# A state space layer's tables M, loaded from overlapping parts of K's rows instead of from a DRAM copy of their own

## The chip, the core and the metric

The kernel runs on one core of a Trainium2 chip. The metric is the device time of one execution in microseconds (us). Five engines work side by side, each in the order of its own instruction list: TensorE (PE; its weight loads are shown as PEld), VectorE (DVE), ScalarE (ACT), GpSimd (POOL) and SyncE (SP). SP does no arithmetic here, it only issues DMAs. Sixteen DMA engines move the data, whichever engine issues the transfer.

## What is computed

A decoder trunk of two layers on 256 tokens of 2048 features, in float32. Layer 0 mixes tokens with a causal convolution module, layer 1 with a state space layer (SSM) that ends in a gated linear unit. Each is followed by a squared-ReLU MLP with 8192 hidden features. The SSM is the part that the change touches:

```python
def ssm_module(h, lam_re, lam_im, log_dt, b_re, b_im, c_re, c_im, d_skip, w_glu):
    u = h.astype(f32).reshape(bsz, L, SSM_GROUPS, SSM_GROUP)      # 128 groups of 16 channels
    ...
    bu_re = jnp.einsum("blgc,gpc->blgp", u, bb_re)                # 64 complex states per group
    ...
    _, _, s_re, s_im = lax.associative_scan(combine, (a_re, a_im, bu_re, bu_im), axis=1)
    y = (jnp.einsum("blgp,gcp->blgc", s_re, c_re.astype(f32))
         - jnp.einsum("blgp,gcp->blgc", s_im, c_im.astype(f32)))
    y = y.reshape(bsz, L, D_MODEL) + d_skip.astype(f32) * h.astype(f32)
    y = jax.nn.gelu(y).astype(h.dtype)
    z = y @ w_glu
    val, gate = jnp.split(z, 2, axis=-1)
    return val * jax.nn.sigmoid(gate)
```

## The kernel before

**The large products.** Every float32 weight is split into a rounded part `hi` and a rest `lo`, and three products are summed on TensorE. Weights come in steps (`add_t`, `add_f`); a step is two halves of 512 KB. `load` (line 105) has SP issue the DMA of a half into a buffer `raw`, of which there are six (line 127). `split` (line 144) makes `hi` on ACT and `lo` on DVE, with four buffers each (line 153). Then TensorE uses the half. `fetch` (line 100) makes every DMA on SP stand behind the fetch before it, so SP's order is the order in which the program asks. A DMA on SP also waits until the one eight places before it has landed.

**The SSM in chunks.** The 256 tokens are cut into 32 chunks of 8 tokens. For each group of 16 channels there are three constant tables of 128 rows by 128 columns: W takes the 8 x 16 inputs of a chunk to the 64 complex states, V takes the carried state to the 8 x 16 outputs, and M takes the inputs of a chunk to the outputs of the same chunk. M depends only on the distance between two tokens. Its row for token offset d (16 rows, one for each channel c) is a window of a longer row K[g, c] of 15 x 16 numbers, and the windows of neighbouring offsets overlap: columns d*16 to d*16 + 128.

**Where the tables are made.** `ssm_prep` (line 1066) puts the work that builds W, V, K and the rotation table R into a list, `bg`, which is worked off between the steps of layer 0's MLP. `kstage` (line 1317) makes K for 8 groups on TensorE, ACT and DVE and writes it to the DRAM tensor Kd of [128 groups, 16 channels, 240] with four DMAs on POOL's queue. `mstage` (line 1334) copies 16 rows of M for 32 groups from Kd to the DRAM tensor Md of [128 rows, 128 groups, 128], also on POOL's queue; with 8 offsets and 4 blocks of 32 groups that is 32 copies.

**Where the tables are used.** The 128 groups are taken in four blocks B = 0 to 3. `table` (line 1394) has SP load a table of one block, [128 partitions, 32 groups, 128 columns] or 2 MB, into one of six large buffers `blk`. The tables W0, W1, M0, V0 and R0, R1 are asked for between the last steps of layer 0's MLP (line 1827). M1, V1, W2 and R2 are asked for in `begin` (line 1585) at the start of the gated unit. The others are asked for just ahead of given steps of the gated unit (`before_load`, line 1677): W3, then M2 and R3, then V2, M3, V3. `ssm_local(B)` (line 1533) multiplies block B's inputs by M, `ssm_carry(B)` (line 1549) adds the product with V, and `ssm_out(B)` (line 1564) transposes the result for the gated unit, whose matmuls (`mm_t`, lines 268 to 270) then use it. In `begin`, `ssm_local(1)` stands on TensorE ahead of the transposes of `ssm_out(0)`; the other calls stand between steps of the gated unit (`todo`, line 1669). The tile framework adds the waits between engines, and its scheduler picks the order where the program leaves it open.

Two other loads go to fewer than 128 partitions: `xJ`, the inputs by chunks, to 32 partitions at a time in pieces of 512 B (line 1364), and in the convolution `R`, shifted rows, to 32 partitions at a time in pieces of 1136 B (line 537, on ACT's queue).

Of the kernel before, what the change touches and what calls it, by code (L numbers as in the profile page):

```python
# [10 lines left out]
F32 = mybir.dt.float32  # L11
# [8 lines left out]
P = 128  # L20
# [8 lines left out]
G, ST, GC = 128, 64, 16  # L29
CH = 8  # L30
# [7 lines left out]
class Trunk:  # L38
# [47 lines left out]
    def add(self, view, shape, consume, pre=None):  # L86
        self.steps.append((view, shape, consume, pre))
# [978 lines left out]
    def ssm_prep(self):  # L1066
        nc, a, bg = self.nc, self.a, self.bg
        add = lambda c, fn: bg.append((c, fn))
        const = self.const
        self.Wd = self.dram.tile([P, G, P], F32, name="Wd")  # L1070
        self.Kd = self.dram.tile([G, GC, 15 * GC], F32, name="Kd")
        self.Md = self.dram.tile([P, G, P], F32, name="Md")
        self.Vd = self.dram.tile([P, G, P], F32, name="Vd")
        self.Bd = self.dram.tile([G, 2, ST, GC], F32, name="Bd")
        self.Rd = self.dram.tile([P, NQ, 1024], F32, name="Rd")
# [1 line left out]
        dma = nc.gpsimd.dma_start  # L1077
# [223 lines left out]
        def vstage(k):  # L1301
            vs = s["bv"][:, 2944:4096].rearrange("p (g d c) -> p g d c", d=9, c=GC)
            g = slice(8 * k, 8 * k + 8)
            c = [s["c12"][:, i, g, :].unsqueeze(2).broadcast_to([P, 8, 8, GC]) for i in range(2)]
            p = [s[x][:, g, :].unsqueeze(3).broadcast_to([P, 8, 8, GC]) for x in ("pr", "pi")]
            v = vs[:, :, 1:9, :]
            self.tt(v, c[0], p[0], ALU.mult)
            n = 4 if k >= 14 else 8
            t = s["bv"][:, 2944 - 128 * n:2944].rearrange("p (g d c) -> p g d c", d=8, c=GC)
            for h in range(0, 8, n):  # L1310
                h = slice(h, h + n)
                self.tt(t, c[1][:, h], p[1][:, h], ALU.mult)
                s["vadd"] = self.tt(v[:, h], v[:, h], t, ALU.add)
            nc.scalar.activation(vs[:, :, 0, :], s["c12"][:, 0, g, :], AF.Copy)
            dma(out=self.Vd[:, g, :], in_=v.rearrange("p g d c -> p g (d c)"))

        def kstage(k):
            vs = s["bv"][:, 2944:4096].rearrange("p (g x) -> p g x", x=9 * GC)
            bs = s["bv"]
            ps = self.bank([P, 2, P], name="kp")  # L1320
            with self.behind(s["vadd"]), self.tc.high_priority(offset=URGENT):
                for gl in range(8):
                    q, hh = gl % 4, gl // 4
                    nc.tensor.matmul(ps[32 * q:32 * q + 32, hh, :], lhsT=bs[:, (8 * k + gl) * GC:(8 * k + gl + 2) * GC],
                                     rhs=vs[:, gl, 0:P], start=hh == 0, stop=hh == 1, skip_group_check=True)
            ks = self.t2([P, 2, P], name="ks")
            nc.scalar.activation(ks, ps, AF.Copy)
            for j in range(2):
                self.stt(ks[:, j, 0:GC], self.m32[:, 0:GC], self.dgl[:, k, j:j + 1], ks[:, j, 0:GC], ALU.mult, ALU.add)
            kd = self.Kd.rearrange("(k h q) c e -> k q c h e", k=16, h=2, q=4)  # L1330
            for q in range(NQ):
                dma(out=kd[k, q, :, :, 7 * GC:15 * GC], in_=ks[32 * q:32 * q + GC])

        def mstage(B, d):
            dma(out=self.Md[d * GC:(d + 1) * GC, 32 * B:32 * B + 32, :],
                in_=self.Kd[32 * B:32 * B + 32, :, d * GC:d * GC + P].rearrange("g c x -> c g x"))
        for k in reversed(range(16)):
            add(12, lambda k=k: vstage(k))
            add(4 if k >= 12 else 3, lambda k=k: kstage(k))
            if k < 12:  # L1340
                for d in range(2 * (k % 4), 2 * (k % 4) + 2):
                    add(0.5, lambda B=k // 4 + 1, d=d: mstage(B, d))
        for d in range(CH):
            add(0.5, lambda d=d: mstage(0, d))


    def ssm_slice(self, n):
# [46 lines left out]
    def table(self, kind, B):  # L1394

        if kind == "R":
            t = self.t4([P, 2, 16, 32], name="R") if B != 2 else self.S[:, 1]
            self.fetch(t.rearrange("p i g j -> p (i g j)"), self.Rd[:, B])
        else:
            t = self.blk_tile([P, 32, P], name=kind + "t")  # L1400
            src = {"W": self.Wd, "M": self.Md, "V": self.Vd}[kind]
            for h in range(0, 32, 16):
                self.fetch(t[:, h:h + 16, :], src[:, 32 * B + h:32 * B + h + 16, :])
        self.tables[kind, B] = t

    def ssm_block(self, b):
# [452 lines left out]
```

## Time and profile before

| | |
|---|---|
| time, median of 3 runs | 1935.12 us (1935.08 to 1935.7) |
| time of the profiled execution | 1935.06 us |
| its span, first to last instruction | 1933.3 us |
| DMA, mean over the span | 242 GB/s, 468.45 MB |
| Md<-Kd, POOL's queue | 32 DMAs of 256 KB, median 7.1 us to landing |
| Mt<-Md, SP's queue | 8 DMAs of 1024 KB, median 8.8 us to landing |
| Wt<-Wd and Vt<-Vd, SP's queue | 8 DMAs of 1024 KB each, median 9.1 and 8.1 us to landing |

The page gives the busy time of each engine as a share of the span. A view by stretches gives, for each stretch, its length, then for each engine the busy time with the count of instructions, then TensorE's clock, the busy share of the 16 DMA engines, and the GB/s they moved. Transfers overlap within an engine, so the share can come out a little over 1. A row of a DMA queue has its packets, the MB, and the time of its packets as a share of 16 engines over the stretch. A timeline row has start and length in us, engine, line, operation, and output<-input; in brackets stands idle time before it and what ended that. "Landing" is from the issue of a DMA to its completion. In a row of DMAs the three numbers are the length of the issue in ns (least, median, most), then come the first and the last start in us.

### The profile page before, as it was taken

The page shows a single profiled execution, that of the slowest core. Times are in us where ns is not written, and L with a number is a line of the kernel's source. Part 1 is how long each engine was busy: PE and PEld are TensorE (multiplying, and loading weights), DVE is VectorE, ACT ScalarE, POOL GpSimd, SP SyncE. Part 2 cuts the span into 40 slices and gives each one's busy share as a digit, 9 for nine tenths or more (in the row PEclk, how much of TensorE's full clock was granted, in tenths as well). Part 3 has the DMA queues.
Part 4 walks back from the last instruction along what each step waited for, and adds up shares of the span by engine and source line. Part 5 has one row for each costly group of instructions (what it writes and reads, how often), then busy time and mean ns, then how long its engine had stood idle before and what let it go on. Part 6 is the DMA issues. An engine that isn't in the chain of part 4 may idle for free.

```text
span 1933.3 us, 30420 instructions
## 1 busy us (share of the span) xinstructions
PE 1915.5 (99%) x11372; PEld 1641.5 (85%) x11372; DVE 1656.2 (86%) x2246; ACT 1124.9 (58%) x1405; POOL 395.6 (20%) x364
## 2 busy tenths in 40 slices
PE   8999999999999999999999999999999999999998
PEld 8999788888888888888888788888888888888887
DVE  6999798899878898988557869679999999999987
ACT  6444555554465565655545446566666666667664
POOL 3899300001021221213101001001111111111100
PEclk9999999999999999999999999999999999999999
DMA  9667468778788888888898978668998998989984
GB/s 247 186 183 217 124 209 251 220 243 270 251 205 251 238 289 233 280 225 278 280 339 302 337 247 219 195 208 229 260 265 228 266 265 239 260 252 254 247 258 145
DMA packets 338675, 468.45 MB, mean 242 GB/s; under 512 B 16801, under 2 KB 218593, under 8 KB 335169
## 3 DMA queue, kind: packets, MB, share of 16 engines
q1 hardware_dynamic: 296464, 364.69, 59.1%
q0 software_dynamic: 38496, 97.27, 21.5%
q10 hardware_dynamic: 3568, 4.56, 0.8%
q8 instruction: 89, 1.46, 0.3%
q14 instruction: 58, 0.48, 0.1%
HBM read 439.93 MB, written 34.91 MB: 246 GB/s over the span
## 4 chain that ended last, share of the span: by engine, by line
PE 96%; DVE 2%; DMA 1%; issue 0%; ACT 0%; POOL 0%; SPq 0%; POOLq 0%; DVEq 0%; ACTq 0%
PE acc L245 24%; PE acc L248 13%; PE acc L268 7%; PE acc L269 7%; PE acc L270 7%; PE mp L760 4%; PE mp L761 4%; PE mp L759 4%; PE acc L257 3%; PE acc L259 3%; PE acc L258 3%; PE acc L278 2%; PE acc L277 2%; PE acc L279 2%; PE mr L760 2%; PE mr L759 2%
## 5 line engine op out<-in xcount | busy, mean ns | idle before, releaser
L156 ACT ACTIVATE hi<-raw 128x1024 fp32r<-128x1024 f32 x634 | 670.9, 1060 | 622.2 <-PE acc L245 201.4
L163 DVE TENSOR_TENSOR lo<-raw,hi 128x1024 fp32r<-128x1024 f32 x573 | 695.6, 1221 | 184.1 <-ACT hi L156 169.7
L245 PE MATMUL acc<-hT,hi 128*128 128x512 f32 x2048 | 516.6, 392 | 0.1
L245 PEld LDWEIGHTS acc<-hT,hi 128*128 128x128 f32 x2048 | 370.8, 189 | 71.0 <-ACT hi L156 1.7
L248 PEld LDWEIGHTS acc<-hT,lo 128*128 128x128 f32 x2048 | 279.4, 190 | 21.1 <-issue 1.2
L248 PE MATMUL acc<-hT,lo 128*128 128x256 f32 x2048 | 287.0, 282 | 0.0
L156 ACT ACTIVATE hi<-sum 128x1024 fp32r<-128x1024 f32 x152 | 161.4, 1062 | 103.2 <-DVE sum L1025 26.9
L163 DVE TENSOR_TENSOR lo<-sum,hi 128x1024 fp32r<-128x1024 f32 x152 | 185.3, 1219 | 23.9 <-ACT hi L156 14.8
L123 POOL DMA_DIRECT2D sum<-in_mlp_w_down_dram x72 | 87.7, 1222 | 548.8 <-DVE v L1034 310.3
L163 POOL TENSOR_TENSOR lo<-raw,hi 128x1024 fp32r<-128x1024 f32 x60 | 144.0, 2414 | 30.2 <-ACT hi L156 24.1
L257 PE MATMUL acc<-hT,hi 128*128 128x256 f32 x512 | 146.2, 286 | 0.9 <-ACT hi L156 0.9
L259 PE MATMUL acc<-hT,lo 128*128 128x256 f32 x512 | 145.4, 286 | 0.2 <-POOL lo L163 0.2
L258 PE MATMUL acc<-hT,hi 128*128 128x256 f32 x512 | 145.5, 285 | 0.0
L1034 DVE SCALAR_TENSOR_TENSOR cv<-vT,cv 128x256 f32<-128x256 f32 x348 | 141.0, 487 | 2.6 <-ACT cv L587 2.2
L760 PE MATMUL mp<-lo,rT 128*128 128x512 f32 x288 | 112.4, 390 | 0.0
L761 PE MATMUL mp<-hi,rT 128*128 128x512 f32 x288 | 112.2, 390 | 0.0
L759 PE MATMUL mp<-hi,rT 128*128 128x512 f32 x288 | 110.4, 390 | 0.0
L257 PEld LDWEIGHTS acc<-hT,hi 128*128 128x128 f32 x512 | 98.9, 193 | 3.4 <-issue 2.1
L259 PEld LDWEIGHTS acc<-hT,lo 128*128 128x128 f32 x512 | 98.4, 193 | 1.7 <-issue 0.8
L258 PEld LDWEIGHTS acc<-hT,hi 128*128 128x128 f32 x512 | 98.8, 193 | 0.9 <-issue 0.8
L269 PE MATMUL acc<-lo,rT 128*128 128x512 f32 x240 | 93.6, 390 | 0.0
L268 PE MATMUL acc<-hi,rT 128*128 128x512 f32 x240 | 93.6, 391 | 0.0
(359 smaller groups left out, 3247.0 us busy)
## 6 DMA issues: line engine op xcount, KB each, us to landing
raw<-in_mlp_w_up_dram SPq DMA_DIRECT2D x256, 512.0 KB, 6.0
raw<-in_mlp_w_down_dram SPq DMA_DIRECT2D x220, 512.0 KB, 5.7
sum<-in_mlp_w_down_dram POOLq DMA_DIRECT2D x108, 512.0 KB, 7.8
raw<-in_conv_w_in_dram SPq DMA_DIRECT2D x128, 256.0 KB, 3.7
raw<-in_ssm_w_glu_dram SPq DMA_DIRECT2D x62, 512.0 KB, 5.0
raw<-in_conv_w_out_dram SPq DMA_DIRECT2D x32, 512.0 KB, 4.2
Vd<-bv POOLq DMA_DIRECT2D x16, 512.0 KB, 5.6
Md<-Kd POOLq DMA_DIRECT2D x32, 256.0 KB, 7.1
```

Source lines behind the costliest of these rows:

```text
L156: self.nc.scalar.activation(hi, sl, AF.Copy)
L163: ins = eng.tensor_tensor(out=lo, in0=sl, in1=hi.bitcast(F32), op=ALU.subtract)
L245: mm(accs[m], lhsT=hi[:, kk, cs[m]], rhs=xT(k0 + kk), start=first and kk == 0, stop=False)
L248: mm(accs[m][:, 0:T], lhsT=lo[:, kk, cs[m]], rhs=xT(k0 + kk)[:, 0, :], start=False, stop=last and kk == 3)
L257: mm(accs[m], lhsT=hi[:, kk, c], rhs=x[:, 0, :], start=first and kk == 0, stop=False)
L258: mm(accs[m], lhsT=hi[:, kk, c], rhs=x[:, 1, :], start=False, stop=False)
L259: mm(accs[m], lhsT=lo[:, kk, c], rhs=x[:, 0, :], start=False, stop=last and kk == 3)
L268: mm(acc[:, b, :], lhsT=ak[:, 0, t], rhs=hi[:, kk, :], start=first and kk == 0, stop=False)
L269: mm(acc[:, b, :], lhsT=ak[:, 0, t], rhs=lo[:, kk, :], start=False, stop=False)
L759: mm(lhsT=F[0], rhs=hi[:, j, :], start=first and half == j == 0, stop=False)
L760: mm(lhsT=F[0], rhs=lo[:, j, :], start=False, stop=False)
L761: self.mm_last = mm(lhsT=F[1], rhs=hi[:, j, :], start=False, stop=half == j == 1)
```

## The change

Md and the 32 copies into it are gone. `table("M", B)` now loads from Kd: eight DMAs on SP's queue, one for each token offset d, each of which fills 16 partitions (d*16 to d*16 + 15) for 32 groups with rows of 128 numbers (512 B) out of K's rows. W and V are loaded as before. `mstage` and its calls in the list `bg` go, and so the list is shorter by 32 entries of cost 0.5.

```diff
-        self.Md = self.dram.tile([P, G, P], F32, name="Md")
...
-        def mstage(B, d):
-            dma(out=self.Md[d * GC:(d + 1) * GC, 32 * B:32 * B + 32, :],
-                in_=self.Kd[32 * B:32 * B + 32, :, d * GC:d * GC + P].rearrange("g c x -> c g x"))
         for k in reversed(range(16)):
             add(12, lambda k=k: vstage(k))
             add(4 if k >= 12 else 3, lambda k=k: kstage(k))
-            if k < 12:
-                for d in range(2 * (k % 4), 2 * (k % 4) + 2):
-                    add(0.5, lambda B=k // 4 + 1, d=d: mstage(B, d))
-        for d in range(CH):
-            add(0.5, lambda d=d: mstage(0, d))
...
             t = self.blk_tile([P, 32, P], name=kind + "t")
-            src = {"W": self.Wd, "M": self.Md, "V": self.Vd}[kind]
-            for h in range(0, 32, 16):
-                self.fetch(t[:, h:h + 16, :], src[:, 32 * B + h:32 * B + h + 16, :])
+            if kind == "M":
+                for d in range(CH):
+                    self.fetch(t[d * GC:(d + 1) * GC],
+                               self.Kd[32 * B:32 * B + 32, :, d * GC:d * GC + P].rearrange("g c x -> c g x"))
+            else:
+                src = {"W": self.Wd, "V": self.Vd}[kind]
+                for h in range(0, 32, 16):
+                    self.fetch(t[:, h:h + 16, :], src[:, 32 * B + h:32 * B + h + 16, :])
         self.tables[kind, B] = t
```

SP's order in `begin`, where M1 is loaded, is this (- before, + now; each row is line, DMA, output<-input, shape of one, and count):

```order
 L103 DMA raw<-in_ssm_w_glu_dram 128x2x512 x2
 L103 DMA xJ<-xs 32x8x128 x8
-L103 DMA Mt<-Md 128x2048 x2
+L103 DMA Mt<-Kd 16x32x128 x8
 L103 DMA Vt<-Vd 128x2048 x2
 L103 DMA Wt<-Wd 128x2048 x2
```

Eight loads to 16 partitions stand in the place of two loads to 128, ahead of V1 and W2 as before; no other row moved.

SP's order a little later, where M2 is loaded between the raw weights of the gated unit, reads alike:

```order
 L103 DMA Wt<-Wd 128x2048 x2
 L103 DMA raw<-in_ssm_w_glu_dram 128x2x512 x2
-L103 DMA Mt<-Md 128x2048 x2
+L103 DMA Mt<-Kd 16x32x128 x8
 L103 DMA R<-Rd 128x1024
 L103 DMA raw<-in_ssm_w_glu_dram 128x2x512 x6
 L103 DMA Vt<-Vd 128x2048 x2
```

R3 and six raw halves stand behind the eight loads, where they stood behind two. M0 and M3 changed in the same way. On TensorE, ACT and DVE the same instructions stand as before; between 600 and 930 us some have changed places with their neighbours, since the list `bg` is shorter.

## The prediction

> **What bounds the kernel now.** I read the page first, then the busy time by stretches, then TensorE, the SP queue and the landing times around the places where a table M is loaded and used. M0 to M3 are the tables of the four blocks.
>
> ```profile
> PE 1915.5 (99%) x11372; PEld 1641.5 (85%) x11372; DVE 1656.2 (86%) x2246; ACT 1124.9 (58%) x1405; POOL 395.6 (20%) x364
> ...
> 260.00:1040.00 780.00, 780.00 (x4187) 659.98 (x4186) 647.08 (x822) 433.17 (x539) 121.73 (x165) 1.00 0.84 254
> 1040.00:1145.00 105.00, 101.75 (x1151) 83.16 (x1150) 81.06 (x99) 49.46 (x67) 2.50 (x7) 1.00 0.87 322
> ```
>
> From 260 to 1040 us TensorE is busy for 780.00 of 780.00 us. The second stretch is the state space layer, where the tables are used: TensorE idles 3.25 us of 105, and the last two columns (DMA share 0.87, 322 GB/s) show transfers near their limit. So time saved on POOL or in transfers before 1040 us ends no wait of TensorE, and what decides is whether M still arrives in time.
>
> **What the change removes.**
>
> ```profile
> L1335 POOL DMA_DIRECT2D Md<-Kd x32: 630/630/648, 685.2 to 934.3; - x32
> ```
>
> That is 32 x 0.63 = 20.2 us of POOL's queue, and 32 x 256 KB read and written, all between 685 and 942 us, under the gapless TensorE. The scheduler also shifts matmuls of 600 to 930 us against each other, the same number as before, on an engine without a gap. I take 0 for both. A gain could at most be part of the 17.8 us (1933.3 - 1915.5) that TensorE idles in the whole span, nearly all of it elsewhere.
>
> **What it adds: a slower load.** A table is 2.10 MB. Before, two DMAs moved it to all 128 partitions, 8 KB in a row for each. Now eight DMAs each fill 16 partitions in pieces of 512 B. The rates to compare:
>
> ```profile
> 1050.00:1062.00 12.00, 10.24 (x202) 8.57 (x191) 11.82 (x17) 6.75 (x14) 0.12 (x1) 1.00 1.01 421
> 1062.00:1068.00 6.00, 6.00 (x28) 4.97 (x27) 5.89 (x7) 2.12 (x2) 0.00 (x0) 1.00 1.01 385
> 10.00:30.00 20.00, 20.00 (x157) 19.95 (x155) 17.88 (x40) 14.50 (x26) 5.43 (x13) 1.00 1.15 286
> 206.00:208.00 2.00, 2.00 (x27) 1.59 (x29) 2.00 (x6) 0.79 (x1) 1.87 (x1) 1.00 1.02 226
> ...
> q10 hardware_dynamic: 414, 0.42, 94.7%
> ...
> q1 hardware_dynamic: 1009, 0.52, 42.9%
> ```
>
> All four windows have the DMA engines full (share over 1). With tables and weights to 128 partitions they move 385 to 421 GB/s; I take 400, or 5.2 us a table. With the first weights, 512 B pieces to 128 partitions, they move 286. At 206 us, where 94.7% is ACT's queue loading R to 32 partitions (line 537, pieces of 1.1 KB), only 226. The last row is the window 1036.4 to 1040.4 with four loads of xJ to 32 partitions, 512 B pieces, one after another with gaps: 0.52 MB / (0.429 x 4 us) = 303 GB/s, a burst of 8 KB per DMA engine each. No row has a large load to 16 partitions. Its bounds: 303 GB/s if the count of partitions costs nothing, and 113 (half of 226) if the sustained rate falls with the partitions below 32. I take 113, because the table is a sustained load, as R is, and 32 partitions with the longer pieces are already slower than 128 with the shorter. A table then takes 18.6 us, 13.4 us more than before.
>
> [...]
>
> **Where 13.4 us per table go.** SP's queue and the table loads' landing times, then the matmuls that use M1, M2, M3:
>
> ```profile
> 975.69 0.81 SPq L103 DMA_DIRECT2D Mt<-Md  x2
> 977.46 13.97 SPq L103 DMA_DIRECT2D raw<-in_mlp_w_down_dram  x6
> ...
> L103 SPq DMA_DIRECT2D Mt<-Md x2: 339/381/423, 975.7 to 976.1; - x2
> ...
> DMA to landing us min/median/max: 7.4/8.5/9.6
> ...
> L103 SPq DMA_DIRECT2D Mt<-Md x2: 436/489/542, 1045.9 to 1046.5; - x2
> ...
> DMA to landing us min/median/max: 5.0/5.9/6.9
> ...
> L103 SPq DMA_DIRECT2D Mt<-Md x2: 421/422/422, 1076.9 to 1077.3; - x2
> ...
> DMA to landing us min/median/max: 12.4/13.5/14.5
> ...
> L103 SPq DMA_DIRECT2D Mt<-Md x2: 338/381/424, 1107.4 to 1107.8; - x2
> ...
> DMA to landing us min/median/max: 8.0/9.6/11.3
> ...
> 1057.64 1.06 PE L1546 MATMUL mv<-Mt,xJ 128*32 128x128 f32 x32
> 1097.84 1.98 PE L1546 MATMUL mv<-Mt,xJ 128*32 128x128 f32 x64
> 1125.60 1.95 PE L1546 MATMUL mv<-Mt,xJ 128*32 128x128 f32 x64
> ```
>
> - M1 is whole at 1046.5 + 6.9 = 1053.4 and needed at 1057.64: slack 4.2, stall 13.4 - 4.2 = 9.2 us. Behind that matmul stand the transposes of block 0's result and with them the whole gated unit, so all of it is lost.
> - M2: whole at 1077.3 + 14.5 = 1091.8, needed at 1097.84: slack 6.0, stall 7.4. Its issue waits for TensorE to free a buffer, so an earlier delay does not lengthen this slack.
> - M3: whole at 1107.8 + 11.3 = 1119.1, needed at 1125.60: slack 6.5, stall 6.9.
> - M0 is needed only at 1049, but the raw weights queue behind it:
>
> ```profile
> 975.12 1.06 ACT L156 ACTIVATE hi<-raw 128x1024 fp32r<-128x1024 f32 x1 [1.66 <-PE acc L270]
> 977.84 1.06 ACT L156 ACTIVATE hi<-raw 128x1024 fp32r<-128x1024 f32 x1 [1.66 <-PE acc L270]
> ```
>
> One half step takes 2.72 us. The raw half issued at 977.46 takes the buffer of the half read at 975.12; six such buffers (line 127) put its own reading at 975.12 + 6 x 2.72 = 991.4. TensorE needs it three halves later (four hi buffers, line 153), at 999.6, so it must land 2.3 us (hi, then lo) before that: 997.3. Now M0 ends at 985.7 + 13.4 = 999.1 and the half 1.3 us (0.52 MB at 400) behind: stall 3.1 us. The halves after it catch up, since 1.3 is below 2.72.
>
> SP itself issues 32 DMAs in place of 8, in the same places of its order. Its rows for 512 B loads bound one:
>
> ```profile
> L103 SPq DMA_DIRECT2D raw<-in_conv_w_in_dram x128: 367/507/1915, 1.2 to 181.5; - x128
> L103 SPq DMA_DIRECT2D xJ<-xs x8: 539/606/1348, 1036.7 to 1045.2; - x8
> ```
>
> Eight at 0.5 to 0.6 us keep SP 3 to 4 us longer per table, and V1, W2 and R2 stand behind M1. A load also waits for the landing of the load eight places before it, so V1 is issued as the pieces of M1 land. I count 0 for both: the DMA engines are still on M1 when SP is through, so what waits is the transfer, counted above; without that cover it would be those 3 to 4 us, within M1's slack.
>
> **TensorE restarts slowly.** After stalls of 7 to 9 us its first matmuls may run as they do at the kernel's start:
>
> ```profile
> 8.52 1.97 PE L299 MATMUL xt<-ident,x 128*128 128x128 f32 x8
> 12.64 0.41 PE L258 MATMUL acc<-hT,hi 128*128 128x256 f32 x1
> 12.85 0.41 PE L259 MATMUL acc<-hT,lo 128*128 128x256 f32 x1
> 15.20 0.28 PE L258 MATMUL acc<-hT,hi 128*128 128x256 f32 x1
> 15.31 0.28 PE L259 MATMUL acc<-hT,lo 128*128 128x256 f32 x1
> ```
>
> Starts are 0.21 us apart at 12.64 and 0.11 to 0.12 at 15.20; the change came at about 13.1, 4.5 us after the steady work from 8.52. The loss is 4.5 x (1 - 0.12/0.21) = 2.0 us. Bounds: 0 to 2.0 for each of the three long stalls; I take 2.0, so 6.0.
>
> **Sum:** 9.2 + 7.4 + 6.9 + 3.1 + 6.0 = 32.6 us on the profiled execution's 1935.06 (0.06 below the median of 1935.12): **1967.7, about 1968 us**. A measurement tells 0.2%, 3.9 us, from no change.
>
> **The rivals.**
>
> - *M still arrives in time (not slower), 0.18.* The piece size and not the partitions sets the rate, as 286 and 303 GB/s would have it: a table takes 7.3 us, 2.1 more, inside every slack: 1935. It decides at 173 GB/s: there a table takes 6.9 us more, and the stalls are 2.7 + 0.9 + 0.4 = 4.0 us. For it: the bursts of xJ. Against it: R's 226.
>  [...]
> - *Half of it, 0.15.* Successive DMAs fill different partitions and partly overlap, at some 150 GB/s: 8.8 us more a table, stalls of 4.6 + 2.8 + 2.3, and one slow restart: 1935.1 + 9.7 + 2.0 = 1947.
> - *No slow restart, 0.17.* 1935.1 + 26.6 = 1962.
> - *The queue stays behind, 0.10.* After M1 the transfers are 13.4 late and TensorE 9.2. I let the 4.2 us vanish in later gaps of the queue; if they don't, M2 and M3 come 4.2 later each, and a little more from M2's own rest: 1968 + 10 = 1978.
> - *Faster, 0.05.* The reordered matmuls or the freed queues save a few us: 1930.
>
> The forecast itself has 0.35. Slower holds 0.35 + 0.15 + 0.17 + 0.10 = 0.77, same 0.18, faster 0.05. The range reaches from 1935, the case of no stall, to 1980.
>
> **What would show it.** Right: the eight loads of M1 land 2.3 us apart, the last near 1067; the M matmuls of blocks 1, 2 and 3 have idle time before them that ends with a DMA; the DMA share stays full while the GB/s fall to about 110; 256 to 1040 us is unchanged but for some 3 us near 1000. Wrong: M1 whole before 1057 us, or landings under 1 us apart; then the partitions do not set the rate and nothing is lost.

## The result, and the profile after

| | before | after |
|---|---|---|
| median of 6 runs | 1935.47 us (1935.08 to 1935.7) | 1978.5 us (1974.57 to 1981.76) |
| ratio, 95% interval | | 1.0221 (1.0207 to 1.0236) |
| profiled execution | 1935.06 us | 1974.57 us |
| its span | 1933.3 us | 1972.8 us |

The change makes the kernel 2.2% slower. The forecast was 1968 us with a range of 1935 to 1980; the median lies near its upper end, and two of the six runs lie above it. The profiled execution of after is the fastest of its six, so the terms below are compared with its 39.5 us, not with the 43 us of the medians.

The busy time of after by stretches (length, then PE, PEld, DVE, ACT, POOL with counts, TensorE's clock, DMA share, GB/s) is, before the layer and during the load of M1:

```profile
260.00:940.00 680.00, 680.00 (x3698) 575.18 (x3697) 590.26 (x762) 385.22 (x478) 93.49 (x122) 1.00 0.80 235
...
1062.00:1066.00 4.00, 1.88 (x48) 1.07 (x40) 3.95 (x7) 1.25 (x3) 0.00 (x0) 1.00 1.22 106
1066.00:1070.00 4.00, 0.00 (x0) 0.00 (x0) 0.32 (x1) 0.00 (x0) 0.00 (x0) 0.80 1.23 108
```

Up to 940 us TensorE is still busy without a gap, so the removed copies change nothing there. At M1 the DMA engines are full (share 1.22) and move 106 to 108 GB/s; from 1066 us on TensorE, ACT and POOL do nothing meanwhile, and VectorE next to nothing. The SP queue of after, and the landing of M1's eight loads, show how long a table takes:

```profile
975.89 12.73 SPq L103 DMA_DIRECT2D Mt<-Kd  x8
...
1052.93 11.11 SPq L103 DMA_DIRECT2D Mt<-Kd  x8
...
1097.98 16.19 SPq L103 DMA_DIRECT2D Mt<-Kd  x8
...
1136.84 18.03 SPq L103 DMA_DIRECT2D Mt<-Kd  x8
...
L103 SPq DMA_DIRECT2D Mt<-Kd x8: 483/514/4224, 1052.9 to 1059.8; - x8
...
DMA to landing us min/median/max: 5.3/13.1/16.5
```

The last load of M1, issued at 1059.8, lands some 16 us later, at about 1076. The TensorE timeline of after shows who waits for the tables (in brackets the idle time ahead and its end), with the matmuls by which the shift is measured:

```profile
1044.76 1.50 PE L235 MATMUL warm<-ident 128*128 128x128 f32 x12
...
1075.97 1.93 PE L1542 MATMUL mv<-Mt,xJ 128*32 128x128 f32 x32 [10.95 <-DMA Mt<-Kd]
...
1090.17 1.96 PE L1553 MATMUL mv<-Vt,SS 128*32 128x128 f32 x64
...
1124.94 3.64 PE L1542 MATMUL mv<-Mt,xJ 128*32 128x128 f32 x64 [5.88 <-DMA R<-Rd]
1141.07 1.98 PE L1553 MATMUL mv<-Vt,SS 128*32 128x128 f32 x64
...
1163.79 3.64 PE L1542 MATMUL mv<-Mt,xJ 128*32 128x128 f32 x64 [8.70 <-DMA Mt<-Kd]
1178.49 1.98 PE L1553 MATMUL mv<-Vt,SS 128*32 128x128 f32 x64
```

The same landmarks in the timeline of before, as far as the prediction did not show them:

```profile
1038.74 1.50 PE L235 MATMUL warm<-ident 128*128 128x128 f32 x12
...
1069.06 1.96 PE L1557 MATMUL mv<-Vt,SS 128*32 128x128 f32 x64
...
1111.65 1.98 PE L1557 MATMUL mv<-Vt,SS 128*32 128x128 f32 x64
...
1138.59 1.98 PE L1557 MATMUL mv<-Vt,SS 128*32 128x128 f32 x64
```

The lateness grows in four steps: 6.0 us at the start of the gated unit (1044.76 - 1038.74), then to 18.3 and 21.1 at M1, 27.1 and 29.4 at M2, 38.2 and 39.9 at M3. The last figure is the difference of the spans (39.5 us) to within 0.4. In each pair the first number holds the wait. The second also holds the slow matmuls behind it: M's matmuls are 0.06 us apart (1.93 us for 32) where before they were 0.03 apart (1.06 for 32). The row of M2 names R3, the DMA behind M2 in the queue; M2's last load was issued at 1112.5 and took at least 12.1 us to land, so it also ended at about the start of these matmuls, and the trace can't tell the two.

### The profile page after: what moved, and what is told of

Read it like the earlier page. It is cut to its first block, busy times and chain, and to the rows that moved or that the text cites. A ratio compares the mean times of both kernels' runs of the same rounds, so it can differ in the third digit from the quotient of the medians.

```text
span 1972.8 us, 30416 instructions
## 1 busy us (share of the span) xinstructions
PE 1925.3 (98%) x11372; PEld 1648.4 (84%) x11372; DVE 1656.2 (84%) x2246; ACT 1124.8 (57%) x1405; POOL 374.6 (19%) x332
## 4 chain that ended last, share of the span: by engine, by line
PE 91%; DMA 4%; SPq 3%; DVE 1%; issue 0%; POOL 0%; ACT 0%; POOLq 0%; DVEq 0%; ACTq 0%
PE acc L245 24%; PE acc L248 12%; PE acc L268 6%; PE acc L269 5%; PE acc L270 5%; PE mp L759 4%; PE mp L761 4%; PE mp L760 4%; PE acc L257 3%; PE acc L259 3%; PE acc L258 3%; SPq L103 3%; PE acc L278 2%; PE acc L277 2%; PE acc L279 2%; PE mr L760 2%
## 5 line engine op out<-in xcount | busy, mean ns | idle before, releaser
L248 PEld LDWEIGHTS acc<-hT,lo 128*128 128x128 f32 x2048 | 279.4, 190 | 21.1 <-issue 1.2
L156 ACT ACTIVATE hi<-sum 128x1024 fp32r<-128x1024 f32 x152 | 161.5, 1062 | 101.6 <-DVE sum L1025 29.3
L163 POOL TENSOR_TENSOR lo<-raw,hi 128x1024 fp32r<-128x1024 f32 x60 | 144.1, 2415 | 30.4 <-ACT hi L156 27.1
```

Of the source, the lines that this page charges most:

```text
L156: self.nc.scalar.activation(hi, sl, AF.Copy)
L163: ins = eng.tensor_tensor(out=lo, in0=sl, in1=hi.bitcast(F32), op=ALU.subtract)
L248: mm(accs[m][:, 0:T], lhsT=lo[:, kk, cs[m]], rhs=xT(k0 + kk)[:, 0, :], start=False, stop=last and kk == 3)
```

## The experiments

Each ran beside the kernel before on the same chip; the ratios are to that kernel. In the runs that read M from Md, the rate at M1 is read from the same view (stretches) at the same place, 1050 to 1054 us, where loads of M1 are still landing and those of V1 stand behind them on the queue.

**Eight loads of 16 partitions with long pieces.** M comes from Md again, but 16 partitions at a time, 16 KB in a row for each.

```diff
-            for h in range(0, 32, 16):
-                self.fetch(t[:, h:h + 16, :], src[:, 32 * B + h:32 * B + h + 16, :])
+            if kind == "M":
+                for p in range(0, P, 16):
+                    self.fetch(t[p:p + 16], src[p:p + 16, 32 * B:32 * B + 32, :])
...
```

> The kernel before with Md and its copies, but M loaded from Md by eight DMAs of 16 partitions each, 16 KB in a row for a partition. Theory (the count of partitions that one DMA fills sets the rate): as after, about 106 GB/s, the pieces of M1 2.3 us or more apart, SP held 10 to 18 us per table, about 1975 us. Rival (pieces of 512 B set the rate, or their many descriptors on SP): over 300 GB/s, SP held under 5 us, 1935 to 1940 us.

```profile
1050.00:1054.00 4.00, 4.00 (x83) 3.62 (x76) 3.96 (x5) 3.34 (x6) 0.13 (x1) 1.00 0.97 115
```

115 GB/s, 1964.6 us, ratio 1.0147 (1.0132 to 1.0163). Pieces 32 times as long lift the rate by less than a tenth, so the rival that blames the pieces for the rate falls. But the time is 10 us better than I expected and 14 better than after. The TensorE timeline of this run at M1, whose wait is in two parts:

```profile
1056.16 0.64 PE L1561 MATMUL mv<-Vt,SS 128*32 128x128 f32 x16 [1.39 <-DVE SS L1534]
...
1062.12 0.41 PE L1561 MATMUL acc<-Vt,SS 128*32 128x128 f32 x4 [3.46 <-issue]
1067.37 1.94 PE L1550 MATMUL mv<-Mt,xJ 128*32 128x128 f32 x32 [4.84 <-DMA Mt<-Md]
```

and the first of these in before:

```profile
1055.31 0.64 PE L1557 MATMUL mv<-Vt,SS 128*32 128x128 f32 x16 [1.40 <-DVE SS L1530]
```

M1's matmuls are 9.7 us late (1067.37 - 1057.64), of which 0.9 (1056.16 - 1055.31) was there ahead of the wait. So M0 costs 0.9 us here where after has 6.0, and M1's stall is 8.9 us where after has 12.3. That is 8.5 of the 9.7 us between the two profiled executions. The issues also hold SP for less time, 7.4 us at M0 and 3.8 at M1, where after has 12.7 and 11.1. Whether the long pieces, the source Md instead of Kd, or SP's time brings this was not separated. Of the 43 us of the medians, then, 29 come with the loads to 16 neighbouring partitions even in long pieces from Md; the other 14 have no cause shown.

**Two loads of 128 partitions in pieces of 512 B.** Md's rows are padded, so that pieces cannot join.

```diff
-        self.Md = self.dram.tile([P, G, P], F32, name="Md")
+        self.Md = self.dram.tile([P, G, P + GC], F32, name="Md")
...
```

> The kernel before with Md's rows padded from 128 to 144 numbers, so that the same two DMAs per table fill all 128 partitions in pieces of 512 B. Theory (partitions): the M1 pair lands within 4 us later than before, no wait for M, 1935 to 1939 us. Rival (pieces of 512 B): a table takes as long as after, about 1975 us.

```profile
1050.00:1054.00 4.00, 4.00 (x64) 3.44 (x52) 3.93 (x5) 3.34 (x7) 0.13 (x1) 1.00 1.16 291
```

291 GB/s, 1935.42 us, ratio 1.0 (0.9991 to 1.001). Short pieces to all partitions cost a quarter to a third of the rate of 385 to 421, and the slack of the tables takes it up.

**Four loads of 32 neighbouring partitions**, from Md, as the first but with 32.

> The kernel before with M loaded from Md by four DMAs of 32 partitions each. Theory (partitions): about twice the rate of after, 210 to 230 GB/s or 9 to 10 us for a table, 4 to 5 more than before, about the slack of M1: 1935 to 1940 us. Rival (pieces of 512 B): 400 GB/s and 1935 us; the landings of the four pieces, 2.3 us or 1.3 us apart, tell the two apart, not the time.

```profile
1050.00:1054.00 4.00, 4.00 (x84) 3.62 (x77) 3.97 (x4) 3.53 (x6) 0.13 (x1) 1.00 1.05 225
...
1091.00:1105.00 14.00, 11.77 (x51) 9.11 (x49) 13.93 (x15) 6.29 (x7) 0.00 (x0) 1.00 1.00 179
```

225 GB/s as expected, but 1949.41 us, ratio 1.0074 (1.0059 to 1.0089), where I expected 1940 at most. The M1 matmuls start 3.9 us late (1061.55 against 1057.64), and at M2 the queue moves only 179 GB/s while TensorE idles 4.7 us; at M3 it idles 1.6. Why the rate at M2 is below 225 is open. I had let half the rate fit into the slacks of 4 to 6.5 us. M1 needed 4.3 us more than before by the rate and M2 more than that.

**The copies kept.** The changed `table`, with Md and `mstage` as before; nothing reads Md.

> The changed kernel with Md and its 32 copies on POOL's queue kept; nothing reads them. Theory (the removal is worth nothing): the same time as after, 1975 to 1980 us. Rival (without the copies the matmuls of 600 to 930 us or the queues lose or gain by the shift): a difference of 2 us or more.

1979.9 us (1975.12 to 1985.35), ratio 1.0228 (1.0204 to 1.0253), against 1978.5 and 1.0221 for after. The difference of 1.4 us is within the scatter of either kernel, so the removal is worth nothing that these runs can tell.

**Every fourth, every eighth partition.** The loads of 32 and of 16 partitions from Md again, but to partitions that are spread. The edit is shown for every eighth.

```diff
-                for p in range(0, P, 16):
-                    self.fetch(t[p:p + 16], src[p:p + 16, 32 * B:32 * B + 32, :])
+                for p in range(8):
+                    self.fetch(t[p::8], src[p::8, 32 * B:32 * B + 32, :])
```

> As the run with four DMAs of 32 partitions each, but a DMA fills every fourth partition (0, 4, 8, ..., then 1, 5, 9, ...) in place of 32 neighbours. [...]

> As the run with eight DMAs of 16 partitions each, but a DMA fills every eighth partition in place of 16 neighbours. [...]

The first row is the kernel with every fourth partition:

```profile
1050.00:1054.00 4.00, 4.00 (x78) 3.62 (x71) 3.97 (x4) 3.34 (x6) 0.13 (x1) 1.00 0.95 348
```

and this is the kernel with every eighth:

```profile
1050.00:1054.00 4.00, 4.00 (x83) 3.62 (x76) 3.97 (x5) 3.44 (x6) 0.12 (x1) 1.00 1.09 234
```

32 spread partitions: 348 GB/s, below the 400 I expected, and 1935.93 us, ratio 1.0004 (0.9994 to 1.0013); 32 neighbours had 225 and lost 14 us. 16 spread ones: 234 GB/s and 1949.25 us, ratio 1.0073 (1.0058 to 1.0088); 16 neighbours had 115. By the count alone the spread ones would have run as the neighbours did, at 225 and about 1949 us and at 115 and about 1964 us. So the count does not set the rate; what counts is which partitions one DMA fills.

The rates measured stand in three steps: 106 to 115 GB/s to 16 neighbours, 225 and 234 to 32 neighbours and to every eighth partition, 348 to every fourth. What puts a set of partitions on its step no run shows. That every fourth would have the rate of before's tables, and every eighth that of 32 neighbours, was my estimate ahead of the runs.

**The same partitions from other rows.** The spread loads also read rows of Md that lie further apart. Here Md's rows are stored so that a load to every eighth partition reads 16 neighbouring rows.

```diff
...
+            md = self.Md.rearrange("(r k) g x -> k r g x", r=8)
+            for h in range(2):
+                dma(out=md[2 * d + h, :, 32 * B:32 * B + 32, :],
+                    in_=self.Kd[32 * B:32 * B + 32, 8 * h:8 * h + 8, d * GC:d * GC + P].rearrange("g c x -> c g x"))
...
+                for r in range(8):
+                    self.fetch(t[r::8], src[16 * r:16 * r + 16, 32 * B:32 * B + 32, :])
```

> As the run with eight DMAs to every eighth partition, but Md's rows are stored in such an order (by 64 smaller copies) that each of these DMAs reads 16 neighbouring rows of Md, as the run to 16 neighbours did. The source is now that of the slow load, the partitions filled are those of the faster one. Theory (the partitions filled set the rate): 200 GB/s and more at M1, 1946 to 1953 us. Rival (where the rows lie in DRAM sets it): about 125 GB/s and 1964 us.

```profile
1050.00:1054.00 4.00, 3.81 (x56) 3.24 (x47) 3.93 (x5) 3.34 (x7) 0.13 (x1) 1.00 1.03 217
```

217 GB/s and 1947.63 us, ratio 1.0065 (1.0048 to 1.0081). With the source of the slow load (115 GB/s) and the destination of the faster one (234), the rate is that of the destination.

**One table alone.** Only M1, then only M0, comes from Kd (`kind == "M" and B in (1,)`, and `(0,)`).

> The kernel before with only M1 loaded from Kd by eight DMAs; M0, M2 and M3 from Md. Theory (each table's delay is its own and the queue catches up): a wait of 11 to 12 us before M1's matmuls, a slow restart of 2.8, no wait for M2 and M3: 1949 to 1951 us. Rival (the queue stays behind after M1): waits at M2 and M3 as well, 1954 to 1958 us.

> The kernel before with only M0 loaded from Kd by eight DMAs; M1, M2 and M3 from Md. Theory (the terms stand apart): the 6.0 us by which after is late at 1040 us, and no more: 1940 to 1942 us. The prediction on record gave this term 3.1 us, 1938. Rival (what M0 costs is made up or repeated later): 1935 to 1937, or over 1944 us.

The TensorE timeline of the kernel with M1 alone:

```profile
1069.79 1.94 PE L1551 MATMUL mv<-Mt,xJ 128*32 128x128 f32 x32 [6.71 <-DMA Mt<-Kd]
...
1083.56 1.95 PE L1562 MATMUL mv<-Vt,SS 128*32 128x128 f32 x64
...
1112.36 1.98 PE L1551 MATMUL mv<-Mt,xJ 128*32 128x128 f32 x64
1126.18 1.98 PE L1562 MATMUL mv<-Vt,SS 128*32 128x128 f32 x64
...
1140.13 1.96 PE L1551 MATMUL mv<-Mt,xJ 128*32 128x128 f32 x64
```

M1 alone: 1949.6 us, 14.4 above before, ratio 1.0072 (1.0057 to 1.0087). The lateness is 12.15 us at the M1 matmuls and 14.5 at M1's product with V and at M2 and M3 (1083.56 - 1069.06, 1112.36 - 1097.84, 1140.13 - 1125.60). No wait follows, so the queue does catch up.

M0 alone: 1942.89 us (1939.77 to 1945.82), 7.3 above before, ratio 1.0036 (1.0023 to 1.0049), a little over the 1940 to 1942 expected. Its profiled execution is the fastest of the five, 1939.77 us:

```profile
1041.76 1.50 PE L235 MATMUL warm<-ident 128*128 128x128 f32 x12
...
1058.33 0.65 PE L1562 MATMUL mv<-Vt,SS 128*32 128x128 f32 x16 [1.40 <-DVE SS L1535]
...
1061.45 1.93 PE L1551 MATMUL mv<-Mt,xJ 128*32 128x128 f32 x32
```

Here M0 costs only 3.0 us up to the start of the gated unit (1041.76 - 1038.74). M1 is in time, but its matmuls are slow all the same (1.93 us for 32), behind a gap of 1.40 us. Before has the same gap at the same place, and its matmuls run at full speed there (1.06 us for 32).

**TensorE kept at work in the waits.** The changed kernel with extra small matmuls ahead of M1's, M2's and M3's, first too many, then fewer.

```diff
-            with self.behind(self.vmm):
+            with self.behind(self.keep_warm(24, self.vmm)):
                 self.ssm_local(1, 0, 4)
...
-            with self.behind(self.mm_last):
+            with self.behind(self.keep_warm({2: 40, 3: 36}[B], self.mm_last)):
                 self.ssm_local(B)
```

> The changed kernel with 80, 64 and 64 more small matmuls on TensorE, at 0.125 us each, just ahead of the matmuls that use M1, M2 and M3, so that TensorE works through most of the wait. Theory (after the waits TensorE runs slowly because it has idled): the M matmuls of blocks 1 to 3 take 0.03 us apart again, and the 6.8 us of slow work that after shows at the three places go: 1970 to 1974 us. Rival (the clock is lower for another cause, or the extra work costs what it saves): 1977 to 1982 us.

> As the run with 80, 64 and 64 extra matmuls, but with 24, 40 and 36, since each turned out to take 0.25 us and not 0.125: 6, 10 and 9 us, a little less than the waits they stand in. Theory (slow restart after idling): the M matmuls at full speed and 5 to 7 us less than after, 1971 to 1974 us. Rival (nothing to be had, the clock is lower for another cause): 1977 to 1981 us.

The first took 1994.34 us. An extra matmul runs 0.25 us, not the 0.125 I took, since each shows as two records (80 as 160), and the block of 80 at M1 alone lasted 19.76 us, longer than the wait it was to fill. With no idle time left ahead of them, the matmuls of all three tables ran at full speed (1.08 us for 32 at M1, 1.96 for 64 at M2 and M3). The TensorE timeline of the second:

```profile
1067.03 7.25 PE L235 MATMUL warm<-ident 128*128 128x128 f32 x48
1075.81 1.08 PE L1542 MATMUL mv<-Mt,xJ 128*32 128x128 f32 x32 [1.53 <-DMA Mt<-Kd]
...
1125.15 3.37 PE L1542 MATMUL mv<-Mt,xJ 128*32 128x128 f32 x64 [3.53 <-DMA R<-Rd]
...
1166.82 1.96 PE L1542 MATMUL mv<-Mt,xJ 128*32 128x128 f32 x64 [2.23 <-DMA Mt<-Kd]
```

At M1 and M3 the matmuls run at full speed (1.08 us for 32, 1.96 for 64, against 1.93 and 3.64 in after). At M2, where 3.53 us of idle time were left, they don't. So the slow matmuls do come from idling. How much idling it takes is open: at M1 2.93 us with every eighth partition were followed by full speed (1.08 us for 32), 2.50 us with the rows together were not (1.65), and the kernel with M0 alone has slow matmuls after a gap that before has too. The time is 1975.24 us (1972.45 to 1977.61), 3.3 below after where I expected 5 to 7, but with scatters of 5 and 7 us that gain is not established; M2 came later here (29.2 us from its first issue to its matmuls, 27.0 in after), and why is open.

**Two queues.** The loads of odd d go to POOL's queue. Their partitions, 16 to 31, 48 to 63 and so on, are disjoint from those of the even ones.

```diff
...
+                    if d % 2:
+                        self.nc.gpsimd.dma_start(out=t[d * GC:(d + 1) * GC], in_=src)
+                    else:
+                        self.fetch(t[d * GC:(d + 1) * GC], src)
```

> The changed kernel with the loads of odd d, to partitions 16 to 31, 48 to 63 and so on, put on POOL's queue, and those of even d left on SP's. [...]

The stretch with M1's loads, and the DMA queues in it (q1 is SP's, q0 POOL's: packets, MB, share of 16 engines):

```profile
1050.00:1062.00 12.00, 2.69 (x69) 2.26 (x61) 10.82 (x14) 1.16 (x2) 0.13 (x1) 0.76 1.13 113
```

```profile
q1 hardware_dynamic: 1196, 0.59, 55.9%
q0 software_dynamic: 228, 0.74, 55.6%
```

1980.12 us, ratio 1.0234 (1.0217 to 1.0251). Both queues are at work, and together they move 113 GB/s, hardly more than the 106 to 108 of one. I had expected near 210 GB/s and 1942 to 1955 us, an estimate by which the rates of two disjoint sets of partitions add up; it falls. The two queues together fill the 16 engines (share 1.13). What holds them to this rate was not separated.

## Why the prediction was right, and where its sizes were off

- **What bounds, and what the removal is worth.** Right. TensorE is busy 680 of 680 us up to 940, and the copies kept or removed make no difference that can be told.
- **The slower load.** Right in mechanism: the rate falls to a quarter (106 to 108 GB/s against 385 to 421) since a load fills 16 neighbouring partitions. I had put it on the count of partitions; the spread loads show that it is which partitions. For 16 neighbours both give the same figure, so that my 113 held was luck in this respect: for 16 spread partitions it would have been half of what was measured. 113 GB/s was a little high: 106 to 108 in the clear stretch.
- **M1's stall, 9.2 us: measured 12.3 (18.3 - 6.0).** From the first issue to the matmuls it took 23.0 us (1075.97 - 1052.93), where 18.6 and the 2.3 us by which before's M1 (7.5 us) exceeded its 5.2 make 20.9: 2.1 more. Its first issue also came 1.0 later against TensorE (lateness 7.0 at 1052.93, 6.0 at 1044.76). 9.2 + 2.1 + 1.0 = 12.3.
- **M2's stall, 7.4: measured 6.0 (27.1 - 21.1). M3's, 6.9: measured 8.8 (38.2 - 29.4).** M2 took 12.1 us more than before instead of 13.4 (27.0 from first issue to use, against 14.9 to landing), M3 15.3 (26.9 against 11.7).
- **M0, 3.1 us: measured 6.0 in this execution.** This is the term that was furthest off in proportion. It left out that a short stall can cost more than itself. The TensorE timeline of after:

```profile
999.42 0.39 PE L270 MATMUL acc<-hi,rT 128*128 128x512 f32 x1
1001.60 0.50 PE L268 MATMUL acc<-hi,rT 128*128 128x512 f32 x1 [1.78 <-ACT hi L156]
1002.85 0.50 PE L269 MATMUL acc<-lo,rT 128*128 128x512 f32 x1 [0.76 <-DVE lo L163]
...
1004.12 0.63 PE L270 MATMUL acc<-hi,rT 128*128 128x512 f32 x1
1004.55 0.63 PE L268 MATMUL acc<-hi,rT 128*128 128x512 f32 x1
...
1007.53 0.39 PE L270 MATMUL acc<-hi,rT 128*128 128x512 f32 x1
1007.76 0.39 PE L268 MATMUL acc<-hi,rT 128*128 128x512 f32 x1
...
1030.52 1.09 PE L1379 MATMUL ut<-ident,xr 128*128 128x128 f32 x8 [0.82 <-POOL xr L1367]
```

 The raw half behind M0 is late by about what I had worked out: 1.78 + 0.76 = 2.5 us idle. But then matmuls start 0.43 us apart until 1007 instead of 0.23, a slow restart that I had given only to the three long stalls. From 1000 to 1008 us 17 matmuls run where before 37 did; the 20 that are missing, at 8 us / 37 each, are 4.3 us, the idle time included. Of the other 1.7 us of the 6.0, 0.8 is a wait for POOL's xr at 1030.52, which before does not have; 0.9 I did not take apart. The 6.0 is one execution's figure: at the same landmark M0 costs 3.0 us in the kernel with M0 alone, 5.6 and 8.4 in the two with extra matmuls, and 7.4 in the one with the copies kept, though M0 is loaded alike in all of them. The forecast's 3.1 lies at the low end of that.
- **The slow restart, 2.0 each: measured 2.8, 2.3 and 1.7** (the second number of each pair minus the first). The extra matmuls show that idling brings it on, though not how much. That all of it is on the path is supported by the timeline of after; the run meant to win it back left this open.
- **SP's issue time.** Wrong in size. I had 3 to 4 us more per table; eight loads hold SP for 11 to 18. Whether that costs anything is not shown: after M1's last issue the engines are still full with M1 (share 1.23 at 1066 to 1070), as argued, but the kernel with 16 neighbours and long pieces, where SP is held for less at M0 and M1, loses 8.5 us less there.
- **The rivals.** "M still in time" rested on the pieces setting the rate; 291 GB/s to 128 partitions and 115 with long pieces to 16 refute it. "Half of it" needed 150 GB/s and falls by the 106 to 108. "No slow restart" falls by the matmuls behind the three waits. "The queue stays behind" named 1978, near the median, but for another reason: M1 alone leaves no wait at M2 and M3.

By the trace the sum is 6.0 + 15.1 + 8.3 + 10.5 = 39.9 us, where the prediction had 3.1 + 11.2 + 9.4 + 8.9 = 32.6.

## What to carry to other kernels

Before a copy in DRAM is left out, look at what shape of load its layout allows: here the copies cost nothing that can be told, and the load without them ran at a quarter of the rate (106 to 108 GB/s against 385 to 421) on the path. For a load, look at which partitions one DMA fills before looking at the length of its pieces; 32 spread partitions cost no more time here than 128 (1935.93 us against 1935.16), 32 neighbours lost about half the rate (225 GB/s), and a second queue gave nothing back (113 GB/s and 1980.12 us). The pieces and the source can still matter once such a load is on the path: 14 of the 43 us went with long pieces from the copy. And price a TensorE stall with the slow matmuls behind it: 1.7 to 2.8 us here behind waits of 6 to 11 us. After gaps of 1.4 to 3 us they came in some executions and not in others.

## What the runs showed of the hardware beyond that

- Issuing can hold SP for long: eight loads of 256 KB to 16 neighbouring partitions held it for 11.1 to 18.0 us in pieces of 512 B (a single issue for up to 4.2 at M1) and for 3.8 to 15.9 in pieces of 16 KB, where two loads of 1 MB took 0.8 to 1.0.
- The granted clock of after reads 1.00 in the stretch 1062 to 1066, then 0.80 and 0.50 in 1066 to 1070 and 1070 to 1074, where TensorE does nothing: it goes down within the stall itself.
- The kernel that waits for transfers scatters by 7 us (1974.57 to 1981.76). The one before scatters by 0.6 beside it and by 2.6 over all its runs here (1934.59 to 1937.19).
